# A decoder step on one core: where the second norm's square, root and scaling stand in ScalarE's order

## The chip, the cores and the metric

The kernel runs on one core of one Trainium2 chip. The metric is device time in microseconds (us) for one execution, the median of three runs. The engines are named as in the profile: PE (TensorE), DVE (VectorE), ACT (ScalarE), POOL (GpSimd) and SP, which issues the DMAs. Each engine takes its instructions in the order in which the program lists them.

## The reference

One layer of a decoder for 2048 prompt rows and 32 sample rows of width 1024, all in fp32. What matters here stands behind the attention and gating part, whose two head groups come concatenated:

```python
def _rmsnorm(x, g):
    xf = x.astype(jnp.float32)
    y = xf * lax.rsqrt(jnp.mean(xf * xf, axis=-1, keepdims=True) + EPS)
    return (y * g.astype(jnp.float32)).astype(x.dtype)

def _swiglu(x, g, w_gate, w_up, w_down):
    h = _rmsnorm(x, g)
    return (jax.nn.silu(h @ w_gate) * (h @ w_up)) @ w_down
...
    x = x + jnp.concatenate([att, u * gate], axis=-1) @ w_out
    x = x + _swiglu(x, norm2_g, w_gate, w_up, w_down)
```

The output is RMS-normalised once more. The second norm, inside `_swiglu`, is the one that the change touches.

## The kernel before

Matmuls run on pairs of fp32r values: an fp32 operand is split into a high part (ACT copies it to fp32r) and a low part (the rest, subtracted on DVE or POOL), and three products stand for one. The prompt's 16 tiles of 128 rows pass the second half of the layer in three blocks of 6, 6 and 4 tiles; the last block takes the 32 sample rows along as a tile of its own.

For each block the output projection is made in two halves of 512 columns. The first half runs for all tiles, then `second_phase` walks over the tiles: for each it calls `norm2_slot`, and then issues the 24 matmuls of the second half (L1429 to L1431). Slot `k` works on two tiles at once:

- `cur = order[k - 1]`, whose second half has just been summed. `out_end` adds it to the residual row (L1440, DVE). `norm2_square` squares and sums it on ACT (L1468, half a row, where the first half was squared earlier by L1461; L1473, a whole row, for the others). `rms_b` makes the variance (L1449 and L1450, DVE) and its root (L1451, ACT). `rms_c` refines the root by `newton` (L142 to L146, DVE). `norm2_scale` scales the row into a `pair` buffer (L1480, ACT).
- `x = order[k - 2]`, scaled one slot earlier. `Operands` transposes it on PE into two banks `ps_t` (L1492, 8 instructions), and makes the seven operands of a fast matrix product (Strassen's kind) from them. `first`: two ACT copies (L1506, L1507) and five DVE differences (L1508 to L1512). `second`: an ACT split (L135) with its low part on POOL (L138), and an ACT copy of the second bank (L1517). `third`: another ACT split (L135), low part on POOL (L138). `last`: a low part on DVE (L1525).

Slot 1 has only `cur`; the slot behind the last tile comes one step into the products, and the last tile's `Operands` are spread over later steps. The program is written out in order by hand: `later` and `tick` queue further work by step (among it the conversion of the first weights: L1586, L1601 to L1610, and the splits L1617 on ACT, L1621 on POOL or DVE), and each engine takes what it is given in that order. PE's matmuls of the products are L1680 to L1682, of the down projection L1760.

Of the kernel before, what the change touches and what calls it, by code (L numbers as in the profile page):

```python
# [65 lines left out]
def hymba_step(ctx: ExitStack, tc: tile.TileContext, A: dict, O: dict):  # L66
# [73 lines left out]
    def newton(r, v):  # L140

        dve.reciprocal(r, r)  # L142
        if r.shape[-1] == 1:
            dve.tensor_scalar(v, v, r, r, op0=OP.mult, op1=OP.mult)  # L144
            dve.tensor_scalar(v, v, -0.5, 1.5, op0=OP.mult, op1=OP.add)
            dve.tensor_scalar(r, r, v, None, op0=OP.mult)  # L146
            return
        dve.tensor_mul(v, v, r)
        dve.tensor_mul(v, v, r)
        dve.tensor_scalar(v, v, -0.5, 1.5, op0=OP.mult, op1=OP.add)  # L150
        dve.tensor_mul(r, r, v)
# [14 lines left out]
    def zn_tile():  # L166
        return rp.tile([P, 512], F32, name="zn", tag="zn", bufs=3)
# [1047 lines left out]
    for h in range(H):  # L1215
# [4 lines left out]
        if end:  # L1220

            x = s0 - NI
# [26 lines left out]
    for i, it in enumerate(items):  # L1249
        x, h, n = B0 + i, it["h"], it["n"]  # L1250
# [66 lines left out]
    def square_tile():  # L1317
        return pair_tile(F32).rearrange("p a b -> p (a b)")
# [118 lines left out]
    def out_end(B, i, half, ps):  # L1437
        hs = slice(half * 512, (half + 1) * 512)
        if B.rows[i] == P:
            dve.tensor_add(B.acc[i][:, hs], B.acc[i][:, hs], ps)  # L1440
        else:
            tmp = zn_tile()[0:SR]
            act.activation(tmp, ps[SR:2 * SR, :], AF.Copy)
            dve.tensor_add(B.acc[i][0:SR, hs], B.acc[i][0:SR, hs], ps[0:SR])
            dve.tensor_add(B.acc[i][0:SR, hs], B.acc[i][0:SR, hs], tmp)

    def rms_b(s1, n, more=None):
        if more is not None:
            dve.tensor_scalar(s1[:n, 0:1], s1[:n, 0:1], more[:n], None, op0=OP.add)  # L1449
        dve.tensor_scalar(s1[:n, 1:2], s1[:n, 0:1], 1.0 / D, EPS, op0=OP.mult, op1=OP.add)  # L1450
        act.activation(s1[:n, 2:3], s1[:n, 1:2], AF.Sqrt)  # L1451

    def rms_c(s1, n):
        v, r = s1[:n, 1:2], s1[:n, 2:3]
        newton(r, v)
        return r
# [6 lines left out]
    def norm2_square(B, i, junk):  # L1463

        n = B.rows[i]
        s1 = B.s1.get(i)
        if s1 is not None:
            act.activation(B.X[0][:, i, 0:512] if junk is None else junk, B.acc[i][:, 512:1024], AF.Square, accum_out=s1[:, 3:4])  # L1468
            return s1, s1[:, 3:4]
        s1 = fl.tile([P, 4], F32, name="s1", tag="s1", bufs=6)  # L1470
        if n != P:
            B.xn[i] = fc.tile([P, D], F32, name="xns", tag="acc5")
        act.activation(B.X[0][:, i, 0:D] if n == P else B.xn[i][:n], B.acc[i][:n], AF.Square, accum_out=s1[:n, 0:1])  # L1473
        return s1, None

    def norm2_scale(B, i, r):
        n = B.rows[i]
        if n == P:
            B.xn[i] = square_tile()
        act.activation(B.xn[i][:n], B.acc[i][:n], AF.Copy, scale=r)  # L1480
# [46 lines left out]
    def place_staged(B):  # L1527

        for z, eng in enumerate((act, dve)):
            src = B.staged[z].rearrange("p (m i c) -> p i m c", m=28, i=B.nt)  # L1530
            dst = B.X[z].rearrange("p i (m w) -> p i m w", m=28)[:, :, :, 64:]
            if z:
                dve.tensor_copy(dst, src)
            else:
                act.activation(dst, src, AF.Copy)

    def norm2_slot(B, k, order):

        n = len(order)
        cur = order[k - 1] if 1 <= k <= n else None  # L1540
        x = None
        if k == n and B.last:
            place_staged(B)
        if cur is not None:
            if cur in B.open:
                open_end(B, cur)
            out_end(B, cur, 1, B.half1.pop(cur))
        if 2 <= k:
            x = Operands(B, order[k - 2])
            x.first()  # L1550
        if cur is not None:
            s1, more = norm2_square(B, cur, zn_tile() if k == n and B.last else None)
        if x:
            x.second()
        if cur is not None:
            rms_b(s1, B.rows[cur], more)
            r = rms_c(s1, B.rows[cur])
        if x:
            x.third()
        if cur is not None:  # L1560
            norm2_scale(B, cur, r)
        if x:
            x.last()

# [243 lines left out]
    B = blocks[0]  # L1810
# [24 lines left out]
    def open_end(B, i):  # L1835
        out_end(B, i, 0, B.open.pop(i))
# [71 lines left out]
    def second_phase(B, order, after=None):  # L1908

        for k, i in enumerate(order):  # L1910
            norm2_slot(B, k, order)
            B.half1[i] = ps = ps_o()
            for c in range(2):
                tick()
                if c and k > 2 and i in B.open:
                    first_end(B, i)
                out_part(B, i, 1, range(c * 4, c * 4 + 4), ps, c == 0, c == 1)
            if after:
                after(i)
        later(1, norm2_slot, B, len(order), order, ahead=True)  # L1920
        last = {}

        def last_operands(*steps):
            if not last:
                last["x"] = Operands(B, order[-1])
            for step in steps:
                getattr(last["x"], step)()

        for n, steps in ((5, ("first",)), (6, ("second",)), (7, ("third", "last"))):
            later(n, last_operands, *steps, ahead=True)  # L1930
# [284 lines left out]
```

## Time and profile before

| | |
|---|---|
| three runs, median (lowest to highest) | 2535.84 us (2529.48 to 2545.74) |
| the profiled execution, its own time | 2539.89 us |
| its span, first to last instruction | 2538.1 us |
| mean granted TensorE clock | 0.991 |
| busy in the span: PE, DVE, ACT, POOL | 2452.0, 1431.8, 1221.0, 1378.7 us |
| all L1480 (17), start of first and last | 950.7, 2140.0 us |
| ACT idle before L1480, until DVE's L146 | 9.7 us in 17 |
| DVE idle before L1508, until ACT's L1507 | 12.9 us in 12 |

A row of the timeline gives an instruction's start and length in us, its engine, its line, what it writes and reads with their shapes, and in brackets how long its engine stood idle before it and what ended that. Times count from the start of the span. Buffer numbers are left out of the names.

### The profile page before, as it was taken

Reading aid. Unit: us, or ns where it says so; the run is one execution under the profiler, and the core shown is the slowest. Engines: PE = TensorE matmul, PEld = TensorE weight load, DVE = VectorE, ACT = ScalarE, POOL = GpSimd, SP = SyncE. Lnnn points to the kernel's source line nnn. Section 1 sums busy time; section 2 is a strip of 40 time slices with the busy share of each in tenths; the row PEclk is TensorE's granted clock in tenths of the full one; section 3 lists DMA queues with packets and bytes.
Section 4 is the critical chain, followed back from the end, with each engine's and each line's share of the span. In section 5 each row is a group of like instructions: output and inputs, shape, how many; then the busy total and the mean of one; then the engine's idle time right before and its main releaser. Section 6 shows DMA issues by size and latency. Waiting matters only on the chain. (4 is left out here: it accounts for less than half of the span.)

```text
span 2538.1 us, 38943 instructions
## 1 busy us (share of the span) xinstructions
PE 2452.0 (97%) x13598; PEld 2169.2 (85%) x13598; DVE 1431.8 (56%) x2775; ACT 1221.0 (48%) x2579; POOL 1378.7 (54%) x1078
## 2 busy tenths in 40 slices
PE   9999989999999899999999999999999999999996
PEld 7787867778888878999999988999999988999996
DVE  4379785347888866444444475444444466444445
ACT  6424344446877747545545456323323236344432
POOL 1136653133667657767767644644635434776662
PEclk9999999999999999999999999999999999999998
DMA  8864944787787674645536463653644553665553
GB/s 273 248 185 133 297 127 133 245 264 235 199 237 232 169 208 150 212 156 168 198 133 211 147 207 116 217 186 136 217 149 169 192 169 125 224 212 194 195 189 109
DMA packets 313585, 480.00 MB, mean 189 GB/s; under 512 B 25889, under 2 KB 178882, under 8 KB 307502
## 3 DMA queue, kind: packets, MB, share of 16 engines
q1 hardware_dynamic: 308428, 469.00, 57.9%
q10 hardware_dynamic: 4962, 8.51, 1.2%
q8 instruction: 108, 1.77, 0.3%
q14 instruction: 87, 0.71, 0.1%
HBM read 381.72 MB, written 165.83 MB: 216 GB/s over the span
## 5 line engine op out<-in xcount | busy, mean ns | idle before, releaser
L1621 POOL TENSOR_TENSOR op<-fr,op 128x512 fp32r<-128x512 f32 x393 | 499.2, 1299 | 278.5 <-ACT op L1617 264.7
L1682 PE MATMUL ps_m<-xh,op 128*128 128x384 f32 (+5 forms) x1932 | 610.2, 316 | 0.2
L1680 PE MATMUL ps_m<-xh,op 128*128 128x384 f32 (+5 forms) x1932 | 610.1, 316 | 0.0
L1681 PE MATMUL ps_m<-xl,op 128*128 128x384 f32 (+5 forms) x1932 | 609.2, 315 | 0.0
L1760 PE MATMUL ps_o<-dw,hw 128*128 128x512 f32 x2040 | 481.4, 391 | 5.1 <-DVE acc L1762 5.1
L1760 PEld LDWEIGHTS ps_o<-dw,hw 128*128 128x128 f32 x2040 | 380.1, 188 | 84.7 <-DVE acc L1762 8.4
L1762 DVE TENSOR_TENSOR acc<-acc,ps_o 128x512 f32<-128x512 f32 (+1 forms) x362 | 247.8, 687 | 220.5 <-PE ps_o L1760 220.4
L1680 PEld LDWEIGHTS ps_m<-xh,op 128*128 128x128 f32 x1932 | 363.8, 188 | 4.0
L1681 PEld LDWEIGHTS ps_m<-xl,op 128*128 128x128 f32 x1932 | 363.7, 188 | 3.5
L1682 PEld LDWEIGHTS ps_m<-xh,op 128*128 128x128 f32 x1932 | 363.6, 188 | 0.8 <-POOL op L1621 0.8
L1727 ACT ACTIVATE ps_t<-zn 128x384 f32<-128x384 f32 (+2 forms) x132 | 60.0, 454 | 459.4 <-DVE zn L1710 346.2
L1617 ACT ACTIVATE op<-fr 128x512 fp32r<-128x512 f32 x396 | 235.3, 623 | 19.4 <-DMA fr<-ab_d 14.1
L138 POOL TENSOR_TENSOR dw<-fd,dw 128x1024 fp32r<-128x1024 f32 x65 | 156.2, 2403 | 120.1 <-ACT dw L135 119.2
L323 PE MATMUL ps_s<-wh,xh 128*128 128x512 f32 x480 | 195.3, 407 | 6.1 <-ACT xh L135 6.0
L324 PE MATMUL ps_s<-wl,xh 128*128 128x512 f32 x480 | 190.3, 396 | 2.6 <-DVE wl L226 2.6
L325 PE MATMUL ps_s<-wh,xl 128*128 128x512 f32 x480 | 189.7, 395 | 0.0
L1737 ACT ACTIVATE hw<-ps_t 128x384 fp32r<-128x384 f32 (+2 forms) x132 | 57.7, 444 | 176.6 <-DVE ps_t L1733 175.6
L1621 POOL TENSOR_TENSOR op<-pair,op 128x512 fp32r<-128x512 f32 x63 | 81.2, 1295 | 100.2 <-ACT op L1617 96.0
L323 PEld LDWEIGHTS ps_s<-wh,xh 128*128 128x128 f32 x480 | 91.4, 190 | 35.2 <-issue 7.5
L324 PEld LDWEIGHTS ps_s<-wl,xh 128*128 128x128 f32 x480 | 91.7, 191 | 22.2 <-DVE wl L226 5.3
L325 PEld LDWEIGHTS ps_s<-wh,xl 128*128 128x128 f32 x480 | 91.2, 190 | 19.9 <-DVE xl L138 0.3
L621 POOL TENSOR_TENSOR vl<-kv,vh 100x512 fp32r<-100x512 f32 (+1 forms) x32 | 42.9, 1341 | 108.5 <-ACT vh L615 71.7
(486 smaller groups left out, 4788.1 us busy)
## 6 DMA issues: line engine op xcount, KB each, us to landing
fr<-ab_d SPq DMA_DIRECT2D x308, 256.0 KB
fd<-in_w_down_dram SPq DMA_DIRECT2D x66, 512.0 KB
out_ks_dram<-in_cache_k_dram SPq DMA_DIRECT2D x56, 512.0 KB
out_vs_dram<-in_cache_v_dram SPq DMA_DIRECT2D x56, 512.0 KB
ab_d<-fr SPq DMA_DIRECT2D x88, 256.0 KB
raw<-in_w_in_dram SPq DMA_DIRECT2D x72, 256.0 KB
qk_d<-pair SPq DMA_DIRECT2D x64, 256.0 KB
ab_d<-pair SPq DMA_DIRECT2D x63, 256.0 KB
```

Of the source, the lines that this page charges most:

```text
L138: (eng_lo or pool).tensor_sub(lo, src, hi.bitcast(F32))
L323: pe.matmul(o[j], xh[:, k, :], wh, start=(k == 0), stop=False)
L324: pe.matmul(o[j], xh[:, k, :], wl, start=False, stop=False)
L325: pe.matmul(o[j], xl[:, k, :], wh, start=False, stop=(k == KD - 1))
L1617: act.activation(ops[f, j][0], ab[f][j], AF.Copy)
L1621: (pool if f or j else dve).tensor_sub(lo_, ab[f][j], hi.bitcast(F32))
L1680: pe.matmul(out, wh[:, ks], xh[:, :, k], start=(k == 0), stop=False)
L1681: pe.matmul(out, wh[:, ks], xl[:, :, k], start=False, stop=False)
L1682: pe.matmul(out, wl[:, ks], xh[:, :, k], start=False, stop=(k == 3))
L1727: act.activation(g, c, AF.Silu)
L1760: pe.matmul(ps[0:nr], l_, r_[:, cs], start=(z == 0 and y == 0), stop=(z == FC - 1 and y == len(pairs) - 1))
L1762: dve.tensor_add(B.acc[i][0:nr, cs], B.acc[i][0:nr, cs], ps[0:nr])
```

## The change

`norm2_slot` issues the same calls in another order. The square of `cur` moves ahead of `x.first()`; the variance and its root move ahead of `x.second()`; the refinement and the scaling stay between `x.second()` and `x.third()`, but `x.third()` and `x.last()` change places behind them, so that the third split comes last.

```diff
         if 2 <= k:
             x = Operands(B, order[k - 2])
-            x.first()
         if cur is not None:
             s1, more = norm2_square(B, cur, zn_tile() if k == n and B.last else None)
         if x:
+            x.first()
+        if cur is not None:
+            rms_b(s1, B.rows[cur], more)
+        if x:
             x.second()
         if cur is not None:
-            rms_b(s1, B.rows[cur], more)
-            r = rms_c(s1, B.rows[cur])
-        if x:
-            x.third()
-        if cur is not None:
-            norm2_scale(B, cur, r)
+            norm2_scale(B, cur, rms_c(s1, B.rows[cur]))
         if x:
             x.last()
+            x.third()
```

Only ACT's order differs. First place: ACT in slot 5 of block 0 (tile `acc_10305`, its sums `s_10447`; the transposed tile is in `ps_t_10463` and `ps_t_10468`), before:

```order
L1461 ACTIVATE zn,s_10447<-acc_10305 128x512
L1506 ACTIVATE zn<-ps_t_10463 128x256
L1507 ACTIVATE xh_9920<-ps_t_10463 128x256
L1468 ACTIVATE xh_9920,s_10447<-acc_10305 128x512
L135 ACTIVATE xh_9920<-zn 128x512
L1517 ACTIVATE xh_9920<-ps_t_10468 128x512
L1451 ACTIVATE s_10447<-s_10447 128x1
L135 ACTIVATE xh_9920<-zn 128x512
L1480 ACTIVATE pair<-acc_10305,s_10447 128x1024
```

and in the changed kernel:

```order
L1461 ACTIVATE zn,s_10447<-acc_10305 128x512
L1468 ACTIVATE xh_9920,s_10447<-acc_10305 128x512
L1506 ACTIVATE zn<-ps_t_10463 128x256
L1507 ACTIVATE xh_9920<-ps_t_10463 128x256
L1451 ACTIVATE s_10447<-s_10447 128x1
L135 ACTIVATE xh_9920<-zn 128x512
L1517 ACTIVATE xh_9920<-ps_t_10468 128x512
L1480 ACTIVATE pair<-acc_10305,s_10447 128x1024
L135 ACTIVATE xh_9920<-zn 128x512
```

The square L1468 stands ahead of the two copies, the root L1451 ahead of the second split and the copy L1517, and the scaling L1480 ahead of the third split, which is now the last of the slot.

Second place: DVE in the same slot. Before and in the changed kernel it has the same rows in the same order:

```order
L1440 TENSOR_TENSOR acc_10305<-acc_10305,ps_o_10424 128x512
L1508 TENSOR_TENSOR zn<-zn,ps_t_10463 128x256
L1509 TENSOR_TENSOR xl_9921<-ps_t_10463,xh_9920 128x256
L1510 TENSOR_TENSOR zn<-ps_t_10468,zn 128x256
L1511 TENSOR_TENSOR zn<-ps_t_10468,zn 128x256
L1512 TENSOR_TENSOR zn<-ps_t_10468,zn 128x256
L1449 TENSOR_SCALAR s_10447<-s_10447 128x1
L1450 TENSOR_SCALAR s_10447<-s_10447 128x1
L142 RECIPROCAL s_10447<-s_10447 128x1
```

The variance (L1449, L1450) stays behind the five differences L1508 to L1512.

Third place: ACT in block 1, from the scaling of one slot to the scaling of the next (tiles `acc_15847`, `acc_15883`), before:

```order
L1480 ACTIVATE pair<-acc_15847,s_15951 128x1024
L1506 ACTIVATE zn<-ps_t_16283 128x256
L1507 ACTIVATE xh_15487<-ps_t_16283 128x256
L1468 ACTIVATE xh_15487,s_16001<-acc_15883 128x512
L135 ACTIVATE xh_15487<-zn 128x512
L1517 ACTIVATE xh_15487<-ps_t_16288 128x512
L1451 ACTIVATE s_16001<-s_16001 128x1
L135 ACTIVATE xh_15487<-zn 128x512
L1480 ACTIVATE pair<-acc_15883,s_16001 128x1024
```

and in the changed kernel:

```order
L1480 ACTIVATE pair<-acc_15847,s_15951 128x1024
L135 ACTIVATE xh_15487<-zn 128x512
L1468 ACTIVATE xh_15487,s_16001<-acc_15883 128x512
L1506 ACTIVATE zn<-ps_t_16283 128x256
L1507 ACTIVATE xh_15487<-ps_t_16283 128x256
L1451 ACTIVATE s_16001<-s_16001 128x1
L135 ACTIVATE xh_15487<-zn 128x512
L1517 ACTIVATE xh_15487<-ps_t_16288 128x512
L1480 ACTIVATE pair<-acc_15883,s_16001 128x1024
```

Between two scalings there now stand, ahead of the copies that read the transposed tile, the third split of the slot before and the square of this one.

## The prediction

> **What bounds the kernel now.** First the page's table of busy time, then who waited for whom, asked for TensorE (PE) over the first block's norm stage (945 to 1012 us).
>
> ```profile
> PE 2452.0 (97%) x13598; PEld 2169.2 (85%) x13598; DVE 1431.8 (56%) x2775; ACT 1221.0 (48%) x2579; POOL 1378.7 (54%) x1078
> PE ps_t L1492 <- ACT pair L1480: 3.8, 3, 1.6
> ```
>
> PE is busy 97% of the span. Whatever other engines do counts only where PE ends up waiting, and a wait of PE in mid-program is not given back later. In the norm stage PE's only wait is at the transposes (L1492), for ACT's scaling (L1480): 3.8 us in 3 waits. So 3.8 us is about all that a better slot order could win in this block, and the question is whether L1480 comes earlier or later. The timeline shows the transposes (PE, start and length), the wait in brackets:
>
> ```profile
> 974.45 1.09 PE L1492 MATMUL ps_t<-ident,pair 128*128 128x128 f32 x8 [1.54 <-ACT pair L1480]
> 982.62 1.09 PE L1492 MATMUL ps_t<-ident,pair 128*128 128x128 f32 x8 [1.60 <-ACT pair L1480]
> 989.30 1.04 PE L1492 MATMUL ps_t<-ident,pair 128*128 128x128 f32 x8
> ```
>
> These belong to slots 5, 6 and to the last tile. Now slot 5 itself, with the end of slot 4 and the start of slot 6: first ACT, then DVE, then POOL.
>
> ```profile
> 973.25 1.15 ACT L1480 ACTIVATE pair<-acc,s 128x1024 f32<-128x1024 f32 x1 [0.46 <-DVE s L146]
> 975.40 0.64 ACT L1617 ACTIVATE op<-raw 128x512 fp32r<-128x512 f32 x1 [1.00 <-POOL raw L1610]
> 976.45 0.62 ACT L1461 ACTIVATE zn<-acc 128x512 f32<-128x512 f32 x1
> 977.07 0.36 ACT L1506 ACTIVATE zn<-ps_t 128x256 f32<-128x256 f32 x1
> 978.91 0.63 ACT L135 ACTIVATE xh<-zn 128x512 fp32r<-128x512 f32 x1 [0.60 <-DVE zn L1510]
> 980.25 0.19 ACT L1451 ACTIVATE s<-s 128x1 f32<-128x1 f32 x1
> 981.42 1.15 ACT L1480 ACTIVATE pair<-acc,s 128x1024 f32<-128x1024 f32 x1 [0.46 <-DVE s L146]
> 983.38 0.38 ACT L1506 ACTIVATE zn<-ps_t 128x256 f32<-128x256 f32 x1
> ...
> 977.79 0.42 DVE L1508 TENSOR_TENSOR zn<-zn,ps_t 128x256 f32<-128x256 f32 x1 [2.79 <-ACT xh L1507]
> 979.82 0.15 DVE L1450 TENSOR_SCALAR s<-s 128x1 f32<-128x1 f32 x1
> ...
> 974.09 1.27 POOL L1610 TENSOR_TENSOR raw<-fr,raw 128x512 f32<-128x512 f32 x1
> 979.62 2.70 POOL L138 TENSOR_TENSOR xl<-zn,xh 128x512 fp32r<-128x512 f32 x2 [0.48 <-ACT xh L135]
> ```
>
> The loop reads: ACT copies the transposed tile out (L1506, L1507); DVE, which sat idle 2.79 us for it, makes the five differences from L1508 on and only then, in its own fixed order, the variance (L1450); ACT takes the root (L1451), DVE refines it, ACT scales (L1480), and 1.20 us after L1480's start (973.25 to 974.45, 981.42 to 982.62) the next transposes run. From L1506 to L1480 is 4.35 us. The square (L1468) is not on this chain today: the five differences cover it.
>
> **The change, part by part.** It adds and removes no instruction. The orders of PE, DVE, POOL and SP stay as they were, so no DMA moves. Three groups move in ACT's order, in each slot that has both halves.
>
> *The square goes ahead of L1506.* DVE still makes the variance behind its five differences, and these wait for L1507. So the square only delays the chain's head. The price is what a 512-wide square with its accumulator read holds ACT: 0.62 us (L1461, 976.45, to L1506, 977.07). Where ACT gets there before the add L1440, it also waits for that add.
>
> *The root goes ahead of the second split (L135) and L1517.* It then follows L1450 as closely as in slot 1, where nothing was between them. Rows of slots 1 to 3, DVE and ACT in turn:
>
> ```profile
> 947.51 0.69 DVE L1440 TENSOR_TENSOR acc<-acc,ps_o 128x512 f32<-128x512 f32 x1 [1.05 <-PE ps_o L1431]
> 948.29 0.63 ACT L1468 ACTIVATE xh<-acc 128x512 fp32r<-128x512 f32 x1 [1.41 <-DVE acc L1440]
> 949.30 0.15 DVE L1450 TENSOR_SCALAR s<-s 128x1 f32<-128x1 f32 x1
> 949.49 0.20 ACT L1451 ACTIVATE s<-s 128x1 f32<-128x1 f32 x1 [0.47 <-DVE s L1450]
> 952.97 0.69 DVE L1440 TENSOR_TENSOR acc<-acc,ps_o 128x512 f32<-128x512 f32 x1 [1.16 <-PE ps_o L1431]
> 953.40 0.38 ACT L1506 ACTIVATE zn<-ps_t 128x256 f32<-128x256 f32 x1 [1.00 <-PE ps_t L1492]
> 957.73 1.16 ACT L1480 ACTIVATE pair<-acc,s 128x1024 f32<-128x1024 f32 x1 [0.46 <-DVE s L146]
> 960.92 0.68 DVE L1440 TENSOR_TENSOR acc<-acc,ps_o 128x512 f32<-128x512 f32 x1
> 961.51 0.41 DVE L1508 TENSOR_TENSOR zn<-zn,ps_t 128x256 f32<-128x256 f32 x1
> 961.63 1.06 ACT L1473 ACTIVATE xh<-acc 128x1024 fp32r<-128x1024 f32 x1 [1.20 <-DVE acc L1440]
> 965.14 1.15 ACT L1480 ACTIVATE pair<-acc,s 128x1024 f32<-128x1024 f32 x1 [0.46 <-DVE s L146]
> ```
>
> L1450 to L1451 takes 0.19 there and 0.43 in slot 5 (979.82 to 980.25): a gain of 0.24. The second split and L1517 then fill the wait for DVE's refinement. The chain from L1506 to L1480 becomes 4.11.
>
> *The third split goes behind L1480.* L1480 was waiting 0.46 us for DVE anyway, so it gains nothing beyond the 0.24. But the split's 0.52 us (a 512-wide copy; two of L1617 took from 975.40 to 976.45) now stands ahead of the next slot's work on ACT, and its low part on POOL (the second of the two L138) starts only at L1480 + 1.06 (what L1480 holds ACT, 1569.62 to 1570.68 further below) + 0.71 (L135, 978.91, to L138, 979.62) and lasts 1.35. POOL works in order: L1610 behind it, and ACT's L1617 that waits for L1610, move with it.
>
> Block 0, as shifts of L1480. Slot 2: the square starts 0.78 after the add (947.51 to 948.29), so at 953.75, and L1506 at 954.37 instead of 953.40: +0.97 - 0.24 = +0.7. Slot 3 squares the whole row (1.05 us), 0.71 behind an add at 960.92; DVE's queue, some 0.9 late, puts the add at 961.8, L1506 at 963.6 and L1480 (3.9 later, this slot has no L1449) at 967.5: +2.3, that is 1.6 more. Slot 4: ACT is the queue; 0.62 + 0.52 - 0.24 = 0.9 more. Slot 5: L1610 starts 3.12 after L1480 (1.06 + 0.71 + 1.35) instead of 0.84 (973.25 to 974.09), so 2.28 later, which swallows the 0.52; with 0.62 - 0.24 that is 2.7 more. Slot 6: L1506 came 1.96 after L1480 (981.42 to 983.38) and now comes about 3.1 after it, since the buffer it writes is the one that POOL's late low part reads: 1.14 - 0.24 = 0.9 more. Sum 6.8; the last transposes had 0.4 of slack, so PE loses **6.4 us**.
>
> Block 1, a slot in which PE sets the pace, and the last slot:
>
> ```profile
> 1558.18 1.04 PE L1492 MATMUL ps_t<-ident,pair 128*128 128x128 f32 x8
> 1558.38 0.69 DVE L1440 TENSOR_TENSOR acc<-acc,ps_o 128x512 f32<-128x512 f32 x1 [0.90 <-PE ps_o L1431]
> 1558.88 0.38 ACT L1506 ACTIVATE zn<-ps_t 128x256 f32<-128x256 f32 x1 [0.81 <-PE ps_t L1492]
> 1563.27 1.15 ACT L1480 ACTIVATE pair<-acc,s 128x1024 f32<-128x1024 f32 x1 [0.46 <-DVE s L146]
> 1564.54 1.04 PE L1492 MATMUL ps_t<-ident,pair 128*128 128x128 f32 x8
> 1569.62 1.15 ACT L1480 ACTIVATE pair<-acc,s 128x1024 f32<-128x1024 f32 x1 [0.45 <-DVE s L146]
> 1570.68 0.36 ACT L1690 ACTIVATE raw<-ps_m 128x256 f32<-128x256 f32 x1
> 1571.17 1.03 PE L1492 MATMUL ps_t<-ident,pair 128*128 128x128 f32 x8
> ```
>
> PE's own period is 6.36 us. L1480 + 1.20 is 1564.47, so there is 0.07 of slack and no wait. Now L1506 comes at 1558.38 + 0.78 + 0.62 = 1559.78, +0.90, and L1480 +0.66: PE waits 0.6. Further on ACT's queue sets the pace: 1.06 + 0.52 + 0.62 + 4.11 = 6.31 a slot, plus 0.52 for each weight conversion (L1617) between slots, of which two follow slot 2 and one slot 3. That gives +0.7, +0.9, +0.5, +0.1 and +0.4 for the five slots, 2.6; the last slot had 0.35 of slack (1569.62 + 1.20 against 1571.17): **2.2 us**. Block 2 has three full slots of this kind, one conversion and one staged copy between them: 0.7 + 0.4 + 0.5 = **1.6 us**. Its slot for the sample rows stays covered.
>
> Longer PE gaps can also cost clock. Slot 4's L1480 comes at 973.25 + 3.2 and releases the transposes at 977.65; PE's matmuls behind them end at 984.0 (+ 6.36), and slot 5's L1480 (981.42 + 5.9, + 1.20) releases the next at 988.5: a gap of 4.5 us. Ahead of slot 5 the same sum gives 2.6. This trace has a PE gap of 2.88 us, and the four microseconds behind it (length, busy time by engine, granted clock):
>
> ```profile
> 458.60 0.66 PE L341 MATMUL ps_t<-ident,zn 128*128 128x128 f32 x4 [2.88 <-ACT zn L335]
> 459.00:463.00 4.00, 4.00 (x14) 2.94 (x13) 2.29 (x3) 1.68 (x4) 1.35 (x1) 0.57 0.86 279
> ```
>
> At 0.57 those 4 us lose 1.7 us of matmul work. In slot 6 some 0.4 is covered by the wait that follows. I take **0.9 us**, between 0 and 2 x 1.7 if a second gap drops it too. (The Trainium skill, "TensorE: Matmul & The Clock Gate", section "What's actually happening", puts the drop to half rate at an idle window of about 3.4 us. By it a 4.5 us gap is enough and slot 5's gap of 2.6 is not; this trace drops already at 2.88. Going by the page the sum is 11.1 as well, with 12.8 excluded.)
>
> Sum: 6.4 + 2.2 + 1.6 + 0.9 = 11.1. The profiled execution took 2539.89 around a span of 2538.1, so its like would take 2551.0; the median of the runs is 2535.84, and from it I get **2546.9 us**. That is 0.4%, inside the 1% that a measurement of this kernel can about tell.
>
> What the trace does not show is what POOL's lag does where block 0's products start. Its last low part starts 1.77 behind L1480 instead of 0.45 ahead of it (979.62 + 1.35 against 981.42), so 2.2 more than L1480's own 6.8, while PE is 6.4 late. If PE waits for all of it, that is 2.6 more; if the converted weights are far enough ahead, nothing. I take nothing, since PE waited for L1480 alone in this stretch; both ends go into the range. Below, POOL's tow in slot 5 may be half hidden (-1.8), slot 3's add may not slip (-0.9), and the clock may hold (-0.9): +7.5.
>
> **The rivals.** *Not slower*: the root's branch, not the copies, ends last. It decides at L1508: if the differences started no later than now, the square ahead would be free, the root 0.24 earlier and L1480 with it. For it speaks slot 3, where L1508 (961.51) followed the add at once, with no wait for ACT; against it the 2.79 us idle in slot 5, which end at L1507. Five slots of the first block at 0.24 give 1.2 us: 2534.6; the ceiling is the 3.8, 2532.0.
>
> *Tow*: POOL's late third low part does not stop at L1610 but reaches the weight conversions of the first products in every block (2.6 each, 7.8), and both clock drops come (3.4 instead of 0.9): 2535.84 + 11.1 + 7.8 + 2.5 = 2557.2. For it speaks that POOL is in order; against it that POOL is busy only 54% of the span and can catch up.
>
> *No effect*: PE's slack takes it all, as after a wait the next add is early. It holds for single slots of block 1 but not where ACT's queue is the pace. At most +3: 2538.
>
> **How the numbers follow.** Forecast 0.65, tow 0.18, not slower 0.10, no effect 0.07. The runs before spread from 2529.48 to 2545.74, so a median may sit some 6 off. The range is 2536 to 2561: +7.5 less 7 below, 2557.2 plus 4 above; it leaves out most of "not slower" and the far end of tow. Slower by over 1% (above 2561.2) is a quarter of tow, 0.05; faster by over 1% would need 25 us where only 3.8 are waited for, 0.01; within 1% 0.94.
>
> **What would show it.** Right: in block 0 the waits of L1492 for L1480 grow from 3.8 to about 10 us, the largest ahead of slot 6 (about 4); DVE's idle before L1508 grows; L1451 directly behind L1450 (0.19); new waits of some 0.5 us in blocks 1 and 2; L1610 some 3 us behind L1480. Wrong: L1508 no later than now within a slot, waits of L1492 that shrink, or PE waits for L1621 at the first products that are larger than these.

## The result, and the profile after

The changed kernel takes 2552.91 us (median; 2546.43 to 2562.28) against 2534.75 for the kernel before on the same chip (2529.48 to 2545.74): ratio 1.0071, 95% interval 1.0055 to 1.0086, so 18.2 us or 0.7% more. Forecast were 11.1 us more, 2546.9, in a range of 2536 to 2561. The profiled execution took 2562.28 us around a span of 2560.5, at a mean granted clock of 0.986 (before 0.991).

Line numbers behind `norm2_slot` are one lower than before (L1617 is L1616, L1610 is L1609, L1621 is L1620, L1680 to L1682 are L1679 to L1681). First the page's busy times, then what PE waited for, in the first block's norm stage (945 to 1020 us), in block 1's (1525 to 1600) and in block 2's (2120 to 2190):

```profile
PE 2466.2 (96%) x13598; PEld 2181.2 (85%) x13598; DVE 1433.6 (56%) x2775; ACT 1218.9 (48%) x2579; POOL 1377.2 (54%) x1078
...
PE ps_t L1492 <- ACT pair L1480: 8.8, 4, 3.4
...
PE ps_t L1492 <- ACT pair L1480: 1.4, 3, 0.8
...
PE ps_m L1679 <- ACT xh L1535: 1.4, 1, 1.4
PE ps_t L1492 <- ACT xns L1480: 1.0, 1, 1.0
PE ps_t L1492 <- ACT pair L1480: 0.5, 2, 0.3
```

The waits of L1492 for L1480 grew from 3.8 to 8.8 us in block 0, and 1.4 us of them appeared in block 1, as forecast. PE's busy time grew by 14 us although it has the same 13598 matmuls: some of them ran at a lower clock, as the windows below show. The 1.0 us for the sample rows (`xns`) is not new: it was 1.3 before, just ahead of this window. The wait for L1535, the staged copy of the sample rows, was not forecast at all.

To place the time, the distance from one block's first L1480 to the next block's first, and from the last block's to the end of the span, is compared with the same distance before: **block 0 +8.0, block 1 +2.0, block 2 and the rest +11.1**. A shift of 1.3 was there ahead of block 0's first L1480 already, in work that the change does not touch. The 11.1 is on the low side: the profile before has a short drop of the clock behind block 2's first L1480 (0.88 and 0.70 from 2112 to 2120 us, 1.7 us lost) that the changed kernel's profile lacks.

Slot 5 of block 0, where the forecast put the largest delay, after the change; ACT, then DVE, then POOL:

```profile
978.72 1.15 ACT L1480 ACTIVATE pair<-acc,s 128x1024 f32<-128x1024 f32 x1
979.77 0.62 ACT L135 ACTIVATE xh<-zn 128x512 fp32r<-128x512 f32 x1
983.00 0.63 ACT L1616 ACTIVATE op<-raw 128x512 fp32r<-128x512 f32 x1 [2.62 <-POOL raw L1609]
985.29 0.36 ACT L1506 ACTIVATE zn<-ps_t 128x256 f32<-128x256 f32 x1
988.23 0.20 ACT L1451 ACTIVATE s<-s 128x1 f32<-128x1 f32 x1 [2.31 <-DVE s L1450]
989.41 1.15 ACT L1480 ACTIVATE pair<-acc,s 128x1024 f32<-128x1024 f32 x1
...
986.01 0.42 DVE L1508 TENSOR_TENSOR zn<-zn,ps_t 128x256 f32<-128x256 f32 x1 [5.35 <-ACT xh L1507]
988.04 0.15 DVE L1450 TENSOR_SCALAR s<-s 128x1 f32<-128x1 f32 x1
...
980.47 1.27 POOL L138 TENSOR_TENSOR xl<-zn,xh 128x512 fp32r<-128x512 f32 x1 [0.85 <-ACT xh L135]
981.70 1.28 POOL L1609 TENSOR_TENSOR raw<-fr,raw 128x512 f32<-128x512 f32 x1
```

The weight sum L1609 starts 2.98 us behind L1480 (0.84 before), ACT stands idle 2.62 us for it (1.00 before), and from L1506 to L1480 it is 4.12 us (forecast 4.11, before 4.35). DVE waits 5.35 us for ACT instead of 2.79.

At the end of block 2's norm stage stands what the forecast missed. First the staged copies before the change, then the same place after it:

```profile
2135.10 0.58 ACT L1535 ACTIVATE xh<-xst 128x448 fp32r<-128x448 f32 x1 [0.26 <-PE ps_o L1430]
2135.34 0.39 DVE L1533 CAST xl<-xst 128x448 fp32r<-128x448 f32 x1 [1.09 <-PE ps_o L1431]
```

```profile
2144.52 1.15 ACT L1480 ACTIVATE pair<-acc,s 128x1024 f32<-128x1024 f32 x1
2146.27 1.26 POOL L138 TENSOR_TENSOR xl<-zn,xh 128x512 fp32r<-128x512 f32 x1 [0.83 <-ACT xh L135]
2147.57 0.58 ACT L1535 ACTIVATE xh<-xst 128x448 fp32r<-128x448 f32 x1 [1.37 <-POOL xl L138]
2147.57 0.39 DVE L1533 CAST xl<-xst 128x448 fp32r<-128x448 f32 x1 [2.30 <-POOL xl L138]
2148.20 0.33 PE L1679 MATMUL ps_m<-xh,op 128*128 128x136 f32 x1 [1.38 <-ACT xh L1535]
```

DVE's copy writes into `xl`, which POOL's last low part writes too, and ACT's copy into `xh`, which that low part reads; the columns are others, the buffers the same. The low part now comes behind L1480, so both copies wait for it, and PE waits 1.38 us for its first product. The windows of 4 us behind that wait (busy time of PE, PEld, DVE, ACT, POOL, then the granted clock) show what it set off:

```profile
2148.00:2152.00 4.00, 3.80 (x28) 3.80 (x28) 2.60 (x8) 1.41 (x5) 0.00 (x0) 0.81 0.00 0
2152.00:2156.00 4.00, 4.00 (x20) 4.00 (x20) 2.17 (x8) 3.02 (x6) 2.24 (x2) 0.50 0.00 0
...
2164.00:2168.00 4.00, 4.00 (x21) 4.00 (x21) 1.76 (x8) 1.37 (x6) 1.27 (x1) 0.50 0.00 0
2168.00:2172.00 4.00, 4.00 (x25) 4.00 (x25) 0.30 (x1) 1.32 (x3) 2.41 (x2) 0.63 0.04 8
2172.00:2176.00 4.00, 4.00 (x39) 4.00 (x38) 1.18 (x4) 1.88 (x4) 2.27 (x3) 1.00 0.77 253
```

PE waits for nothing there, yet starts 20 matmuls in 4 us instead of 38 or 39: some 20 us at half clock, in the midst of a full queue. The drop does not come at once: the first products still start 0.11 us apart, and only from 2150.5 on 0.21. Summing (1 - clock) x 4 over the six windows from 2148 to 2172 (0.81, four times 0.50, 0.63) gives **10.2 us** of lost work. Before the change the same matmuls ran at 1.00:

```profile
2140.00:2144.00 4.00, 4.00 (x38) 4.00 (x38) 2.66 (x9) 2.10 (x5) 0.95 (x1) 1.00 0.02 4
```

### The profile page after: what moved, and what is told of

Its sections match the earlier page's. It is cut to its first block, busy times and chain, and to the rows that moved or that the text cites. A ratio compares the mean times of both kernels' runs of the same rounds, so it can differ in the third digit from the quotient of the medians.

```text
span 2560.5 us, 38944 instructions
## 1 busy us (share of the span) xinstructions
PE 2466.2 (96%) x13598; PEld 2181.2 (85%) x13598; DVE 1433.6 (56%) x2775; ACT 1218.9 (48%) x2579; POOL 1377.2 (54%) x1078
## 5 line engine op out<-in xcount | busy, mean ns | idle before, releaser
L1620 POOL TENSOR_TENSOR op<-fr,op 128x512 fp32r<-128x512 f32 x393 | 499.5, 1299 | 280.9 <-ACT op L1616 265.0
L1679 PE MATMUL ps_m<-xh,op 128*128 128x384 f32 (+5 forms) x1932 | 614.7, 318 | 1.4 <-ACT xh L1535 1.4
L1681 PE MATMUL ps_m<-xh,op 128*128 128x384 f32 (+5 forms) x1932 | 614.5, 318 | 0.1
L1680 PE MATMUL ps_m<-xl,op 128*128 128x384 f32 (+5 forms) x1932 | 613.5, 318 | 0.0
L1679 PEld LDWEIGHTS ps_m<-xh,op 128*128 128x128 f32 x1932 | 368.3, 191 | 5.7 <-ACT xh L1535 1.6
L1680 PEld LDWEIGHTS ps_m<-xl,op 128*128 128x128 f32 x1932 | 368.0, 190 | 3.5
L1681 PEld LDWEIGHTS ps_m<-xh,op 128*128 128x128 f32 x1932 | 367.9, 190 | 0.8 <-POOL op L1620 0.8
L1616 ACT ACTIVATE op<-fr 128x512 fp32r<-128x512 f32 x396 | 235.4, 623 | 19.2 <-DMA fr<-ab_d 15.2
L1620 POOL TENSOR_TENSOR op<-pair,op 128x512 fp32r<-128x512 f32 x63 | 81.2, 1297 | 99.9 <-ACT op L1616 95.7
L1691 DVE TENSOR_TENSOR raw<-zn,ps_m 128x384 f32<-128x384 f32 (+1 forms) x63 | 32.5, 516 | 122.7 <-PE ps_m L1681 69.4
```

What stands on the lines that cost most here:

```text
L1616: act.activation(ops[f, j][0], ab[f][j], AF.Copy)
L1620: (pool if f or j else dve).tensor_sub(lo_, ab[f][j], hi.bitcast(F32))
L1679: pe.matmul(out, wh[:, ks], xh[:, :, k], start=(k == 0), stop=False)
L1680: pe.matmul(out, wh[:, ks], xl[:, :, k], start=False, stop=False)
L1681: pe.matmul(out, wl[:, ks], xh[:, :, k], start=False, stop=(k == 3))
```

## The experiments

The theory behind the result: three costs, namely the square ahead of the copies (blocks 0 and 1), POOL's late low part that tows the weight sum (slot 5 of block 0), and the staged copies' wait with the long stretch at half clock. The rival: the square is the whole cost, and the clock falls for another reason. All ratios are to the kernel before, on the same chip in the same runs; they weigh all executions and lie near the ratio of the means, so they can differ a little from that of the medians. "Period" is the distance from one L1480 to the next. The columns by block come from one profiled execution each, in us against before, as defined above; they leave out what lies ahead of block 0, which differs by -5.4 to +3.9 us. Short drops of the clock, 1.7 us lost in each, come at changing places from one profiled execution to the next, so these columns scatter: where two kernels have the same code in a block, they differ by up to 1.3 us. The periods of block 0 in the second table then differ by less than 0.05.

| kernel | block 0 | block 1 | block 2 and rest | ratio (95%) |
|---|---|---|---|---|
| the change | +8.0 | +2.0 | +11.1 | 1.0071 (1.0055 to 1.0086) |
| square alone | +4.4 | +2.1 | +0.6 | 1.0028 (1.0016 to 1.0041) |
| third split last alone | +3.9 | +0.9 | +9.6 | 1.0037 (1.0021 to 1.0053) |
| root alone | +3.4 | +0.4 | -0.2 | 1.0021 (1.0012 to 1.0030) |
| square and root | +8.1 | +2.4 | +3.3 | 1.0055 (1.0038 to 1.0072) |
| square and third split | +8.0 | +3.0 | +13.4 | 1.0084 (1.0069 to 1.0098) |
| change, third split back in one slot | +8.3 | +3.0 | +2.2 | 1.0052 (1.0035 to 1.0068) |
| change, gap filled with matmuls | +9.3 | +2.3 | +3.8 | 1.0059 (1.0039 to 1.0078) |
| before, root between second split and L1517 | +0.0 | -0.3 | -1.3 | 1.0010 (0.9997 to 1.0023) |
| before, scaling early | +4.0 | -0.1 | -0.7 | 1.0021 (1.0008 to 1.0035) |
| third split last, low part on DVE | +4.5 | +1.7 | +0.9 | 1.0030 (1.0015 to 1.0045) |
| before, gap of 1.4 us | +0.1 | -0.1 | +10.4 | 1.0021 (1.0007 to 1.0035) |
| before, gap of 3.3 us | +0.2 | -0.1 | +8.7 | 1.0048 (1.0031 to 1.0064) |

And the periods of block 0's slots 2 to 6 against before (7.00, 7.41, 8.11, 8.17, 6.34 us), beside the forecast:

| kernel | 2 | 3 | 4 | 5 | 6 | sum |
|---|---|---|---|---|---|---|
| forecast for the change | 0.7 | 1.6 | 0.9 | 2.7 | 0.9 | 6.8 |
| the change | 0.71 | 2.52 | 0.90 | 2.52 | 0.58 | 7.23 |
| square alone | 0.95 | 1.90 | 0.61 | 0.67 | 0.51 | 4.64 |
| third split last alone | -0.01 | -0.30 | 0.52 | 2.15 | 0.35 | 2.71 |
| root alone | 0.23 | 0.61 | 0.20 | 1.03 | 0.65 | 2.72 |
| square and root | 1.16 | 2.49 | 0.80 | 1.65 | 0.50 | 6.60 |
| square and third split | 0.95 | 1.61 | 1.13 | 2.78 | 0.82 | 7.29 |

### Square alone

```diff
         if 2 <= k:
             x = Operands(B, order[k - 2])
-            x.first()
         if cur is not None:
             s1, more = norm2_square(B, cur, ...)
         if x:
+            x.first()
             x.second()
```

> Only the square moves to the front of the slot; root, scaling and third split stay where they were before. Theory (three separate costs: square, tow by the late third low part, staged copies): block 0 loses 0.97 in slot 2, about 1.6 in slot 3, 0.6 in slots 4 and 5, little in slot 6, so about 4; block 1 about 1.4; block 2 about 0.9; no tow, no long stretch at half clock; L1535 waits as before. Sum +6, ratio 1.0025. Rival (the square is the whole cost, the late third split costs nothing of its own): nearly the whole +18, ratio 1.007.

Measured 2543.32 us against 2537.64, ratio 1.0028; block 0 +4.4, block 1 +2.1, block 2 and the rest +0.6, and no long stretch at half clock. The theory's sizes stand and the rival falls: the square is some 7 us of the whole.

### Third split last alone

```diff
-        if x:
-            x.third()
         if cur is not None:
             norm2_scale(B, cur, r)
         if x:
             x.last()
+            x.third()
```

> Only the third split moves, behind the scaling and the last low part; square and root stay as before. Theory: slots 2 and 3 of block 0 do not change, slot 4 +0.5, slot 5 +2.3 (POOL L1610 about 3 us behind L1480), slot 6 +1.1, together about 3.6 for PE; block 1 +0.4; at block 2's end the staged copies wait for POOL's late low part, some 1.4 us of PE, and the granted clock then falls to 0.5 for some 20 us, 8 us lost. Sum +14, ratio 1.0055; without the long clock drop +6, ratio 1.0024. Rival (the square is the cost): within 2 us of before.

The profiled execution shows both: slot 5 +2.15, and in block 2 a wait of 1.3 us for L1535 with 10.2 us lost at half clock behind it. But the ratio came out at 1.0037, between the two expected values. The twelve executions suggest why: nine had a mean clock of 0.985 to 0.988 and took 2546.0 to 2551.6 us, three had 0.991 to 0.994 and took 2534.9 to 2541.0. So the long stretch seems to come in most executions and not in all; only the profiled ones show it directly.

### Which part of the wait costs

The change with the third split back ahead of the scaling in the one slot before the staged copies:

```diff
+            r = rms_c(s1, B.rows[cur])
+        early = B.last and k == n - 1
+        if x and early:
+            x.third()
+        if cur is not None:
+            norm2_scale(B, cur, r)
         if x:
             x.last()
-            x.third()
+            if not early:
+                x.third()
```

> The changed kernel, but in the one slot ahead of the staged copies the third split goes back in front of the scaling. Theory: blocks 0 and 1 as in the changed kernel (+8, +2.3); L1535 no longer waits for POOL, PE does not wait ahead of the first product of block 2, the granted clock stays at 1.00 there, and block 2 loses 1 to 2 us instead of 10.5: about 9 us below the changed kernel, ratio to before 1.0037. Rival (the drop in clock at block 2 comes from something else, such as the total load): as the changed kernel, ratio 1.007.

The change with PE kept at work in the gap:

```diff
+        if B.last and f == 0 and a == 0 and q == 0:
+            for _ in range(12):
+                pe.matmul(whole, wh[:, 0:P], wl[:, 0:n], start=True, stop=True)
         for k in range(4):
```

> The changed kernel with 12 more matmuls of 136 columns ahead of block 2's first product, into the same bank, which the product then overwrites; they read converted weights only and need not wait for the staged copies, so PE works (12 x 0.113 = 1.36 us) while it waited 1.38. Theory (the idle gap of 1.4 us sets off the 20 us at half clock): the clock stays at 1.00, about 8 us below the changed kernel although PE does more, ratio 1.004. Rival (the clock falls because of the narrow matmuls or of the load, not of the gap): the drop stays, time as the changed kernel or 1 us more, ratio 1.007.

The staged copy's row and the clock behind it when the third split is back (the copy still waits 0.59 us, PE no longer for it), then PE and the clock when the gap is filled:

```profile
2146.90 0.58 ACT L1535 ACTIVATE xh<-xst 128x448 fp32r<-128x448 f32 x1 [0.59 <-POOL xl L138]
...
2148.00:2152.00 4.00, 4.00 (x38) 4.00 (x38) 2.40 (x9) 1.75 (x6) 0.00 (x0) 1.00 0.00 0
```

```profile
2150.65 1.54 PE L1679 MATMUL ps_m<-op 128*128 128x136 f32 x12
...
2152.00:2156.00 4.00, 3.90 (x35) 3.75 (x35) 2.62 (x8) 1.51 (x5) 0.00 (x0) 1.00 0.00 0
2156.00:2160.00 4.00, 3.28 (x30) 3.13 (x30) 2.29 (x9) 3.68 (x8) 2.14 (x2) 1.00 0.00 0
```

In both profiled executions the stretch is gone. With the gap filled, L1535 waited 1.39 us for POOL as in the change, the first product came as late, and PE did twelve matmuls more; yet block 2 and the rest fell from +11.1 to +3.8. So what is expensive is that PE stands idle, not the lateness of the copy. By their ratios the two are 4.8 and 3.0 us below the change, less than the 9 and 8 expected and with intervals that overlap the change's, so a saving in the time of all executions is not shown. What a stretch costs where it is seen (10.2 us) seems to be more than what it costs on average.

### A gap without the change

The kernel before, with the staged copy on ACT issued four times, and in a second kernel seven times:

```diff
-                act.activation(dst, src, AF.Copy)
+                for _ in range(4):
+                    act.activation(dst, src, AF.Copy)
```

> The kernel before, with the staged copy on ACT (L1535) issued four times instead of once, so that TensorE alone gets a gap ahead of block 2's first product: no split is moved, no low part is late. The three more copies hold ACT some 0.55 us each, the last ends near 2137.3 against transposes that end near 2136.1: a gap of about 1.2 us, and the last slot of block 2 up to 1.7 us later. Theory (a gap of little over 1 us at this place sets off about 20 us at half clock in most executions): the profiled run shows the stretch at 0.50, a loss of 8.5 us beside 1 to 2 us of delay, median about +8, ratio 1.003. Rival (the drop needs the changed order, for instance POOL's and DVE's idle time): only the delay, +1 to +2, ratio 1.0006, clock 1.00.

> As the run with the staged copy issued four times, but seven times: a gap of about 2.8 us ahead of block 2's first product. If the length of the half-clock stretch follows from the gap, it is twice as long as after 1.4 us (40 us, 17 us lost, ratio 1.008). If the gap only sets it off, the stretch is again about 20 us with 8.5 lost, and the time is 1.6 us above the run with four copies, ratio 1.004.

The first product's wait (its line is L1681 here) and the granted clock behind it, with four copies, then with seven:

```profile
2132.21 0.33 PE L1681 MATMUL ps_m<-xh,op 128*128 128x136 f32 x1 [1.43 <-ACT xh L1536]
...
2136.00:2140.00 4.00, 4.00 (x21) 4.00 (x21) 1.49 (x5) 1.32 (x2) 1.27 (x1) 0.50 0.00 0
...
2148.00:2152.00 4.00, 4.00 (x20) 4.00 (x20) 1.63 (x8) 1.24 (x5) 1.27 (x1) 0.50 0.00 0
2152.00:2156.00 4.00, 4.00 (x24) 4.00 (x24) 0.30 (x1) 1.32 (x3) 2.50 (x2) 0.61 0.07 8
```

```profile
2135.56 0.48 PE L1681 MATMUL ps_m<-xh,op 128*128 128x136 f32 x1 [3.25 <-ACT xh L1536]
...
2136.00:2140.00 4.00, 4.00 (x21) 4.00 (x21) 3.24 (x12) 2.78 (x8) 1.94 (x2) 0.50 0.00 0
...
2148.00:2152.00 4.00, 4.00 (x33) 4.00 (x33) 3.07 (x9) 2.86 (x5) 1.28 (x1) 0.86 0.00 0
```

No split is moved in these kernels, and the stretch is there: 10.2 us lost behind a gap of 1.43, 6.8 behind one of 3.25. The gap sets it off, and a longer gap did not make it longer. The ratio of the short gap, 1.0021 or some 5 us, is again less than its profiled execution's 10.4 us. The fourteen profiled executions of this case agree: the five with a gap of 1.26 to 3.25 us ahead of this product have the stretch, and none of the nine with at most 0.84, or with the gap filled, has it.

### Root, and the order that gained on paper

The root between the second split and L1517, all else as before:

```diff
             split_sb(hi[:, 3:5], lo_[:, 3:5], self.sums[0])
+            then()
             act.activation(hi[:, 1:3], self.pts[1], AF.Copy)
...
-            x.second()
+            x.second(lambda: cur is None or rms_b(s1, B.rows[cur], more))
+        elif cur is not None:
+            rms_b(s1, B.rows[cur], more)
         if cur is not None:
-            rms_b(s1, B.rows[cur], more)
             r = rms_c(s1, B.rows[cur])
```

> The kernel before with one move: the variance and its root go between the second split (L135) and the copy L1517, so that the root follows the variance directly; square, scaling and third split stay. DVE's order does not change. Theory (the root is the one part of the change that gains, 0.24 us a slot where the chain sets the pace): periods of slots 2 to 6 of block 0 each 0.2 shorter where L1480 sets the transposes, 0.6 to 1.2 us in all, nothing in blocks 1 and 2, where TensorE sets the pace; ratio 0.9996, not to be told from 1. Rival (ACT's queue, not the chain, is the pace): no period changes by more than 0.1.

The ratio is 1.0010 (0.9997 to 1.0023), so no gain was measured. In the trace the periods of slots 2 to 6 changed by -0.25, +0.01, -0.24, +0.27 and -0.23: the 0.24 is real in three slots, and slot 5 pays one of them back, which leaves 0.44.

The whole norm ahead of the differences, the scaling right behind L1507 and both splits last; only the slot ahead of the staged copies (`front` is false there) keeps the order of the kernel before:

```diff
+        front = not (B.last and k == n - 1)
+        if x and not front:
             x.first()
...
-        if x:
+        if x and not front:
             x.second()
...
         if x:
-            x.third()
+            x.first() if front else x.third()
         if cur is not None:
             norm2_scale(B, cur, r)
         if x:
+            if front:
+                x.second()
+                x.third()
             x.last()
```

> The square and all of the norm (variance, root, refinement) ahead of the differences on DVE, and the scaling right behind the two copies L1506 and L1507; then both splits. The slot ahead of the staged copies keeps the order of before. L1480 comes about 3.2 us behind the add L1440, as in slot 1 where nothing stands between, against 4.9 now. Theory (in-order POOL decides in block 0): the waits of L1492 for L1480 vanish in slots without weight work, but both low parts come 2 us later and tow L1610, slot 5 about 2 us longer, the sum between -2 and +2 in block 0, nothing in blocks 1 and 2; ratio 0.999 to 1.001. Rival (the chain through L1480 alone decides): all 3.8 us of block 0's waits are won, ratio 0.9985.

The ratio is 1.0021 (1.0008 to 1.0035), block 0 +4.0: slot 2 gained 1.61 us, but slot 3 lost 2.43 and slot 5 1.46. The expected bounds for block 0 (-2 to +2) were too low; the kind of the cost, late low parts and a late weight sum in slot 5, was the expected one (ACT stood 2.64 us idle there for POOL's weight sum). One cost more was not expected: in slots 4 and 6 PE waited 1.45 us in the midst of its transposes for DVE's low part L1525, which reads the bank that they write and now comes late. The rival falls. No order tried is measurably faster than the kernel before.

### Undoing the third split, and giving its low part to DVE

In the first kernel `third` goes back in front of the scaling in every slot of the change. In the second, the third split alone is last, with its low part on DVE.

```diff
+            r = rms_c(s1, B.rows[cur])
+        if x:
+            x.third()
+        if cur is not None:
+            norm2_scale(B, cur, r)
         if x:
             x.last()
-            x.third()
```

```diff
-            split_sb(hi[:, 5:7], lo_[:, 5:7], self.sums[1])
+            split_sb(hi[:, 5:7], lo_[:, 5:7], self.sums[1], eng_lo=dve)
```

> The changed kernel with the third split back in front of the scaling in every slot, so square and root stay early and only the move of the third split is undone. Theory (costs add: square alone gave +4.4, +2.1, +0.6 us by block in the trace, the early root gains 0.24 a slot): block 0 periods of slots 5 and 6 fall back to about +0.4 and +0.3, no tow (L1610 within 1 us of L1480), block 0 +3.5, block 1 +1.8, block 2 +0.5, no stretch at half clock, sum +6, ratio 1.0023. Rival (the square ahead already makes POOL late, the third split only adds to it): block 0 stays above +6.

> The kernel with the third split alone moved last (its run gave slots 4, 5, 6 of block 0 +0.5, +2.2, +0.4, and 9.6 in block 2), now with the low part of the third split on VectorE instead of GpSimd in every slot. Theory (GpSimd takes its work in order, and the late low part tows L1610 and so ACT's L1617): slot 5 falls from +2.2 to about +0.5, the split's own 0.52 on ACT; the staged copies wait about 0.8 us less, the gap ahead of block 2's first product shrinks to some 0.6, and the long half-clock stretch is gone in the profiled run; ratio 1.001. Rival (ACT's own split is what costs): slot 5 stays at +2.

The first was a miss: block 0 +8.1 and a ratio of 1.0055 instead of +3.5 and 1.0023. The rival's mark, block 0 above +6, is met, but the square is not what does it: the kernel with the square alone differs from this one only by the root, and has +4.4 (periods 4.64 against 6.60). The early root, which I had as a gain, costs when it stands ahead of the second split and the third split ahead of the scaling. The second run settled the tow: slot 5 went from +2.15 to -0.06, and POOL's weight sum L1609 starts 0.55 us ahead of slot 4's L1480 instead of some 3 behind it, so there the late low part on POOL was the cost, and not ACT's own split. The time only moved: with DVE's queue carrying the low part, slots 3 and 6 became 1.53 and 2.57 longer, and the ratio is 1.0030 (1.0015 to 1.0045), not the expected 1.001. In block 2, PE's wait for L1535 was 0.8 us, and no long stretch followed.

### Where the root gains and where it costs

To settle the miss, two more kernels: the square and the third split without the early root, and the early root alone.

The first, against the kernel with the square alone in front:

```diff
-        if x:
-            x.third()
         if cur is not None:
             norm2_scale(B, cur, r)
         if x:
             x.last()
+            x.third()
```

The second, against the kernel before:

```diff
+        if cur is not None:
+            rms_b(s1, B.rows[cur], more)
         if x:
             x.second()
         if cur is not None:
-            rms_b(s1, B.rows[cur], more)
             r = rms_c(s1, B.rows[cur])
```

> Square to the front and third split last, the root where it stood before. Theory (these two add): periods of slots 2 to 6 of block 0 as the sums of the two single moves, +1.0 +1.6 to 1.9 +1.1 +2.8 +0.6 to 0.9, together about 7.4; block 1 about +3.0; block 2 the wait for the late low part again, with the long stretch in most executions; ratio 1.007 as the changed kernel, so the early root is worth within 1 us there. Rival (the early root costs in the changed kernel as it did without the late third split, 3.7 us in block 0): slots 2 to 6 together below +5.

> Only the root moves, ahead of the second split; the square stays behind the two copies and the third split in front of the scaling. Theory (taken from the run with square and root early: the root makes ACT wait for DVE's variance with the second split queued behind it, so the split, L1517 and the third split run after it and L1480 comes 0.2 later, and POOL's pair of low parts 1.2 later): periods of block 0 +0.2, +0.2 to 0.6, +0.2, +1.0, 0.0, block 0 about +2, block 1 +0.3, ratio 1.001. Rival (the root only gains, as the prediction had it): slots 2, 4, 5 and 6 each -0.24.

The first came as expected: the square and the third split add up slot by slot (0.95, 1.61, 1.13, 2.78, 0.82). The root alone made every slot of block 0 longer, 2.72 us together, slots 2 to 5 as expected; slot 6 (0.65 for 0.0), block 0 (+3.4 for about +2) and the ratio (1.0021 for 1.001) came out higher. ACT and POOL in slot 4, first before:

```profile
970.73 0.63 ACT L135 ACTIVATE xh<-zn 128x512 fp32r<-128x512 f32 x1 [0.60 <-DVE zn L1510]
972.08 0.19 ACT L1451 ACTIVATE s<-s 128x1 f32<-128x1 f32 x1
973.25 1.15 ACT L1480 ACTIVATE pair<-acc,s 128x1024 f32<-128x1024 f32 x1 [0.46 <-DVE s L146]
...
971.44 2.69 POOL L138 TENSOR_TENSOR xl<-zn,xh 128x512 fp32r<-128x512 f32 x2 [2.01 <-ACT xh L135]
```

Then with the root alone:

```profile
971.64 0.20 ACT L1451 ACTIVATE s<-s 128x1 f32<-128x1 f32 x1 [1.70 <-DVE s L1450]
971.75 0.61 ACT L135 ACTIVATE xh<-zn 128x512 fp32r<-128x512 f32 x1
972.27 0.58 ACT L1517 ACTIVATE xh<-ps_t 128x512 fp32r<-128x512 f32 x1
972.75 0.62 ACT L135 ACTIVATE xh<-zn 128x512 fp32r<-128x512 f32 x1
973.27 1.14 ACT L1480 ACTIVATE pair<-acc,s 128x1024 f32<-128x1024 f32 x1
...
972.44 2.51 POOL L138 TENSOR_TENSOR xl<-zn,xh 128x512 fp32r<-128x512 f32 x2 [3.21 <-ACT xh L135]
```

ACT idles 1.70 us for the variance with the second split behind it, though that split's operand was ready earlier. Three copies then stand between the root and the scaling, so L1480 no longer waits for DVE's refinement but for ACT's own queue, and POOL's first low part starts 0.83 ahead of L1480 (972.44 to 973.27) instead of 1.81 (971.44 to 973.25 before). With the third split moved out from between, the copies fit into the refinement: comparing the change with square and third split, the root gains 0.24, 0.23, 0.26 and 0.24 in slots 2, 4, 5 and 6, and loses 0.91 in slot 3. Root and third split without the square was not tried.

## Why the prediction was right, and where its sum was short

**The block 0 terms stand.** 6.4 and 0.9 of clock were forecast, 8.0 came. Slots 2, 4 and 5 came to within 0.2 us; slot 6 came 0.3 below. In slot 6 the reason given was another than the trace's: L1506 did not wait for POOL's low part to leave a buffer (it starts at 992.21, while that low part runs to 992.43), it came 2.80 us behind L1480 since ACT was busy all that time. The signs were there: L1451 0.19 behind L1450, L1609 some 3 us behind L1480, DVE's idle before L1508 up, waits of L1492 at 8.8 us for about 10. The largest wait was not ahead of slot 6 but 3.4 us ahead of slot 4, since slot 3 came 0.9 longer than forecast (2.52 for 1.6). DVE's weight sum there before, then its rows in the change:

```profile
959.72 0.68 DVE L1607 TENSOR_TENSOR raw<-fr 128x512 f32<-128x512 f32 x1
```

```profile
961.53 1.47 POOL L138 TENSOR_TENSOR xl<-zn,xh 128x512 fp32r<-128x512 f32 x1 [0.83 <-ACT xh L135]
961.77 1.78 DVE L1606 TENSOR_TENSOR raw<-fr 128x512 f32<-128x512 f32 x1
964.78 1.06 ACT L1473 ACTIVATE xh<-acc 128x1024 fp32r<-128x1024 f32 x1 [3.32 <-DVE acc L1440]
```

DVE's weight sum L1606 (L1607 before) lasted 1.78 us beside POOL's low part, against 0.68 in the trace before, where POOL was idle at that time; the adds behind it on DVE, and ACT's square, came later by that. With the early root and the third split ahead of the scaling (root alone, square and root) DVE's low part of a weight, one instruction earlier, lasts 1.76 us beside POOL's (0.68 before). With square and third split but no early root it was the other way about: the same sum took 0.69, and POOL's low part beside it 1.78. The Trainium skill, "SBUF — State Buffer", section "SBUF: two separate sides", says that a VectorE instruction with two SBUF inputs and a GpSimd one that reads SBUF block each other for a whole instruction. These rows agree, with 1.1 and 0.5 us as the price. What slot 3 loses with the early root (0.91, 0.61 and 0.59 us in the three pairs of kernels) fits this meeting of the two engines; no run was made to part it from other causes.

The clock term: short drops came behind both gaps, ahead of slots 5 and 6 (3.2 us of lost work in the windows, by 0.61 at 980 to 984 and 0.75 and 0.83 at 988 to 996), where one was counted on; 1.2 is left in block 0's 8.0 beside the periods (7.23 - 0.4 of slack + 1.2), for 0.9 forecast. That the waits behind them covered the rest is likely, not shown, and the 0.9 was a choice between bounds, so its fit is partly luck.

**Block 1 stands** at 2.0 for 2.2, its five periods at 0.60, 0.89, 0.48, 0.12 and 0.49 for 0.7, 0.9, 0.5, 0.1 and 0.4.

**The block 2 term failed.** 1.6 was forecast and 11.1 came, in the profiled execution. The step said "one staged copy between them" and counted it as 0.5 us of ACT. It did not ask what that copy writes, and so missed its wait for the low part that the same prediction had just made late (L1480 + 1.06 + 0.71, lasting 1.35: from the L1480 at 2144.52 its own sum gives 2147.64 for the end, the trace 2147.53). The wait is 1.38 us; the larger part is the 10.2 us at half clock. The prediction had a clock term, but only for the gaps of block 0, from the one place of the trace where a gap of 2.88 cost 1.7 us. The 18.2 of the medians stand beside 22.4 between the two profiled executions; the changed kernel's was the longest of its six, and the stretch seems to cost less on average. That 2552.91 still lies in the range is partly luck: the upper end made room for conversions towed in every block, which did not come.

**The 0.24 of the root was right for the wrong reason.** Ahead of the second split it holds in slots 2, 4, 5 and 6 with the third split behind the scaling, and not without; between the second split and L1517 it held in three slots without. The prediction took it as a property of the root alone. In block 0 the root nets 0.06 us in the change (7.29 to 7.23). Of the rivals, *not slower* falls (L1508 waits longer for ACT, not less), *no effect* too, and *tow* happened in another place than it had said: PE waits for no converted weight at the first products of block 0, but the late low part did reach the first products of block 2, by way of the staged copies.

## What to carry to other kernels

When a step is moved, list what else touches the buffers it writes, not only what stands behind it in its engine's queue: the costliest waiter here was a copy, one stage later, into another part of the same buffer. Price an idle gap of TensorE by what the clock does behind it (here, in the profiled execution, seven times the gap), and try to fill it where the engine can be given work. Ahead of a wait in an in-order queue, look at what stands ready behind it: an instruction that only moves earlier can still make the next one late.

## What the runs showed of the hardware

The granted clock fell to 0.50 behind gaps of 1.3 to 1.4 us (the change, third split alone, square and third split, the gap kernel: 10.2, 10.2, 12.0 and 10.2 us lost) and stayed there for 20 to 24 us of unbroken matmuls, of 136 and 204 columns in the change. In block 0 of the change the gaps of 2.42 and 2.63 us, ahead of slots 5 and 6, each cost one drop of some 3.4 us at half clock, and the gap of 3.36 ahead of slot 4 none; in block 0 before, gaps of 1.54 and 1.60 us set nothing off. A gap of 0.8 ahead of block 2's first product set nothing off. The Trainium skill, "TensorE: Matmul & The Clock Gate", section "What's actually happening", gives half rate after an idle window of about 3.4 us and full rate again after one busy window. The windows bear out its grain, since the short drops come in steps of 1.7 us lost, half of 3.4; they do not bear out its rule here: 1.4 us of idling was enough, and six such windows of matmuls without a wait passed before the clock came back. Why it stays low so long at this place is open, and so is why not every execution seems to have it. That the gap sets it off is shown by the two kernels that add nothing but a gap; that filling it prevents it rests on one profiled execution.
